# Two edits in a three-block model: modulation sums on VectorE alone, and relative biases written early from 128 partitions

## The chip, the cores and the metric

One core of one Trainium2 chip runs the whole program. The metric is the device time of one execution in microseconds, as the median of several runs. The engines that matter here are TensorE (PE, with its weight loads listed as PEld), VectorE (DVE), ScalarE (ACT), GpSimd (POOL) and the queues that issue transfers: SyncE (SP) for weights, and ACT's own queue for most other loads and stores.

## The reference, cut to what matters

A forward pass of three blocks over 256 tokens of width 1024. Two places of it bear on the change. The first block's attention adds to the scores of head h, query t and key s a bias that depends on the distance t - s alone, looked up in a table of 32 buckets by 8 heads. The third block is modulated by a vector `c` that doesn't depend on the tokens:

```
l_own = einsum('bhqd,bhkd->bhqk', qc, k_own) * scale + bias_h[:, t5_bucket(d_own)]   # block 1
logits = [where(d_own >= 0, l_own, NEG_INF)]
...
cond = silu(c)                                                                       # block 3, c: 1024
for layer in range(2):
    mod = cond @ ada_w[layer] + ada_b[layer]                                         # ada_w[layer]: 1024 x 6144
    shift1, scale1, gate1, shift2, scale2, gate2 = split(mod, 6)
    hn = rmsnorm(x, norm1_w[layer]) * (1 + scale1) + shift1
```

So the modulation is two products of a vector with a matrix of 1024 x 6144, 48 MB of weights in all. Its result is needed only in block 3, but it can be made at any time before.

## The kernel before, in words

Activations lie transposed, 128 features on the partitions, 256 tokens along the row. Nearly every weight matrix is loaded in chunks of 1 MB (128 x 2048 fp32, `wraw`, four buffers named raw, on SP's queue), and each half chunk is split by ACT into a rounded part `hi` (L316) and by DVE into the rest `lo` (L317), four buffers each. PE then does three matmuls of 256 columns for each product (L327 to L329), 48 a chunk. The program is written with a tile framework: each engine has one queue in order, and a scheduler fixes the order of each queue ahead of time. It goes by the order of the lines but may put an instruction ahead of earlier lines when, by its own reckoning, its inputs and its buffer are ready.

`mixers1` (L587) is the first half of block 1. It projects `va` in four chunks (L604 to L612), with the constants loaded at j = 2 (L609), normalises it (L613 to L630), projects `u` (L631 to L636), mixes positions in eight groups (L645 to L653), and then makes the biases (L656 to L668): one matmul picks for 8 heads, on 8 partitions, the 256 bias values by distance; DVE copies them into `bv`, whose tail holds -1e30; a DMA on ACT's queue writes that row of 383 values 128 times for each head into a scratch `relb` in memory; and a second DMA on the same queue reads `rel` (128 x 8 x 256) back with a step that shifts each partition's row by one, so that partition t sees the biases of query t. Then come four chunks each of q and k (L671 to L680), four of v (L681 to L686), and the attention, which first uses `rel` at L701. Large tiles of this stage share nine "wide" buffers of 8 KB per partition.

`peer` (L838) is the second half. Stage "route" selects experts (`chosen`, L859), writes the coefficients to the scratch `coef` and ends with `embed` (L907), which uses w_pp and w_pg. Stage "down" loops over 64 chunks of experts: `ex.down(j)` multiplies the hidden values `gel` with the coefficients (a `slab` is read from `coef` every four chunks, on ACT's queue), splits a chunk of peer_v and does 48 matmuls into four long sums; `ex.up(j + 18)`, as long as j < 46, does the same amount for a later chunk of peer_u; and `ada.step()` does one step of the modulation. Slabs and the accumulator `adaw` share four wide buffers.

`Modulation` (L1391): `start` (L1400) makes `cond` = silu(c) as 128 x 8 in a tile that is kept. There are 48 steps, one for each 1 MB of ada weights. A step loads 128 rows (inputs on the partitions) by 2048 outputs, and DVE adds weight times cond into `adaw` (L1413 for the first of eight, L1415 for the others). After eight steps the column sums are made by PE (`finish`, L1421): 16 matmuls with a block of 128 outputs of `adaw` as weights and a single column of ones, each in two passes of fp32, so 32 weight loads and 32 matmuls of one column (L1426). Six such finishes fill `mod`.

Of the kernel before, what the change touches and what calls it, by code (L numbers as in the profile page):

```python
# [12 lines left out]
F32 = mybir.dt.float32  # L13
# [3 lines left out]
AF = mybir.ActivationFunctionType  # L17
OP = mybir.AluOpType
# [5 lines left out]
D = 1024  # L24
KT = D // 128
NEG = -1e30
LOWEST = -3.0e38
WCH = 2048
# [18 lines left out]
class Pack:  # L47


    def __init__(self):  # L50
        self.parts, self.at, self.n = [], {}, 0
# [71 lines left out]
def tcol(v):  # L123

    return np.asarray(v).reshape(-1, 128).T
# [8 lines left out]
def prepare(**a):  # L134
    a = {k: np.asarray(v) for k, v in a.items()}
    d = {}
    vec = Pack()
    d["xT"] = lay(a["x"][0].T.reshape(D, T), T)[0]
    d["pT"] = lay(a["p"][0, 0].T.reshape(256, T), T)[0]
    w, b = a["w_in"][0], a["b_in"][0]  # L140
    for i, n in enumerate(("u", "va", "q", "k", "vb", "ga", "gb")):
        d["w_" + n] = lay(w[:, i * D:(i + 1) * D], 256)
        if n not in ("va", "vb"):
            vec.add("b_" + n, tcol(b[i * D:(i + 1) * D]))
    d["rows"] = np.stack([b[D:2 * D], b[4 * D:5 * D], a["gmlp_ln_g"][0], a["gmlp_ln_b"][0]])
    d["gm_ws"] = np.ascontiguousarray(a["gmlp_w_s"][0].transpose(2, 0, 1)).reshape(128, -1)
    d["gm_bs"] = a["gmlp_b_s"][0].reshape(1, -1)
    d["w_pa"] = lay(a["w_proj_a"][0], 256)
# [19 lines left out]
    w = a["nsa_w_in_2"][0]  # L168
    o = [0, 1024, 1280, 1536, 1792, 2048, 2304, 2560, 2608]
    q, kc, vc, ks, vs, kw, vw, g = (w[:, o[i]:o[i + 1]] for i in range(8))  # L170
# [13 lines left out]
    d["rows16"][0] = a["fox_b_f_2"][0]  # L184
    d["rows16"][1] = np.concatenate([a["m_i_bias_3"][0], a["m_f_bias_3"][0]])

    vec.add("c", tcol(a["c_3"][0]))
    for l in range(2):
        d[f"ada{l}"] = np.ascontiguousarray(a["ada_w_3"][l].reshape(KT, 128, 3, WCH).transpose(2, 0, 1, 3))
        vec.add(f"ada_b{l}", tcol(a["ada_b_3"][l]))  # L190
        vec.add(f"n1w{l}", tcol(a["norm1_w_3"][l]))
        vec.add(f"n2w{l}", tcol(a["norm2_w_3"][l]))
    vec.add("fnw", tcol(a["final_norm_w_3"]))
    w = a["m_w_in_3"][0]
# [22 lines left out]
class Core:  # L217
# [107 lines left out]
    def mm3(self, ps, w, x, start, stop, **k):  # L325
        mm = self.nc.tensor.matmul
        mm(ps, w[0], x[0], start=start, stop=False, **k)  # L327
        mm(ps, w[0], x[1], start=False, stop=False, **k)  # L328
        mm(ps, w[1], x[0], start=False, stop=stop, **k)  # L329
# [249 lines left out]
def block1(c, x, ada):  # L579
    with c.phase("mix1", 9):  # L580
        hs = mixers1(c, x)
    ada.start()
    with c.phase("peer", 0):
        return peer(c, x, hs, ada)


def mixers1(c, x):  # L587
    nc, d = c.nc, c.d
# [8 lines left out]
    def row(i, eng=nc.scalar):  # L597
        r = c.big([D], nm="row")
        src = d["rows"]
        eng.dma_start(r, bass.AP(tensor=src.tensor, offset=src.offset + i * D, ap=[[0, 128], [1, D]]))  # L600
        return r

    va = c.big([2, D], nm="va")
    for j in range(4):  # L604
        ps = c.tok_chunk(d["w_va"][j], xs, w=None if j else first)
# [4 lines left out]
        f = slice(j * 256, j * 256 + 256)  # L610
# [13 lines left out]
    nc.vector.tensor_scalar(sc[:, :, 3:4], sc[:, :, 3:4], -0.5, 1.5, op0=OP.mult, op1=OP.add)  # L624
    nc.vector.tensor_tensor(sc[:, :, 3:4], sc[:, :, 3:4], sc[:, :, 2:3], op=OP.mult)
    lg, lb = row(2), row(3)
    for i in range(2):
        nc.vector.tensor_scalar(va[:, i], va[:, i], st[:, i, 12:13], sc[:, i, 3:4], op0=OP.subtract, op1=OP.mult)
        nc.vector.tensor_tensor(va[:, i], va[:, i], lg, op=OP.mult)
        nc.vector.tensor_tensor(va[:, i], va[:, i], lb, op=OP.add)  # L630
    u = c.big([KT, T], nm="u")  # L631
    for j in range(4):
        ps = c.lin_chunk(d["w_u"][j], xs)
        for f in range(2):
            g = 2 * j + f
# [6 lines left out]
    src = d["gm_bs"]  # L642
    nc.scalar.dma_start(bs, bass.AP(tensor=src.tensor, offset=src.offset, ap=[[0, 128], [128, 8], [1, 128]]))
    a = (c.big([KT, T], F32R, nm="ahi"), c.big([KT, T], F32R, nm="alo"))
    for g in range(8):  # L645
        ps = c.ms_ps()[:, :256].rearrange("p (n t) -> p n t", n=2)
        for n in range(2):
            nc.tensor.matmul(ps[:, n], va[:, n, g * 128:g * 128 + 128], ws[:, g], start=True, stop=True)
        s = c.small([2, 128], tag="sg")
        nc.vector.tensor_tensor(s, ps, bs[:, g:g + 1, :].to_broadcast([128, 2, 128]), op=OP.add)  # L650
        s = s.rearrange("p n t -> p (n t)")
# [1 line left out]
        c.split(u[:, g], a[0][:, g], a[1][:, g])  # L653


    L = 383  # L656
    ps = c.ms_ps()
    nc.tensor.matmul(ps[:8, :256], c.V("rel_bias")[:32, :], c.C("onehot")[:32, :], start=True, stop=True)
    bv = c.small([384], tag="bv", bufs=1)
    nc.vector.memset(bv[:8, :], NEG)  # L660
    nc.vector.tensor_copy(bv[:8, :256], ps[:8, :256])
    scr = c.dr.tile([8, 128 * L], F32, name="relb")
    nc.scalar.dma_start(scr.rearrange("h (r l) -> h r l", l=L),
                        bv[:8, None, :L].to_broadcast([8, 128, L]))
    rel = c.big([8, 256], nm="rel")
    s = scr[:, :]
    nc.scalar.dma_start(rel, bass.AP(tensor=s.tensor, offset=s.offset + 127,
                                     ap=[[L - 1, 128], [128 * L, 8], [1, 256]]))  # L668


    q, k = c.big([KT, T], nm="q"), c.big([KT, T], nm="k")  # L671
    for j in range(4):
        ps = c.lin_chunk(d["w_q"][j], xs)
        for f in range(2):
            h = 2 * j + f
            nc.vector.tensor_scalar(q[:, h], ps[:, f], c.V("b_q")[:, h:h + 1], 128.0 ** -0.5, op0=OP.add, op1=OP.mult)
        ps = c.lin_chunk(d["w_k"][j], xs)
        for f in range(2):
            h = 2 * j + f
            nc.vector.tensor_scalar(k[:, h], ps[:, f], c.V("b_k")[:, h:h + 1], None, op0=OP.add)  # L680
    vb = c.big([2, D], nm="vb")  # L681
    bvb = row(1)
    for j in range(4):
        ps = c.tok_chunk(d["w_vb"][j], xs)
        f = slice(j * 256, j * 256 + 256)
        nc.vector.tensor_tensor(vb[:, :, f], ps, bvb[:, None, f].to_broadcast([128, 2, 256]), op=OP.add)  # L686
    o = (c.big([KT, T], F32R, nm="ohi"), c.big([KT, T], F32R, nm="olo"))
# [46 lines left out]
    for j in range(4):  # L734
        parts = []
        for gate, proj, src in (("ga", "pa", a), ("gb", "pb", o)):
            ps = c.lin_chunk(d["w_" + gate][j], xs)
            sg = c.small([2, 256], tag="sgm", bufs=3)
            for f in range(2):
                g = 2 * j + f  # L740
                nc.scalar.activation(sg[:, f], ps[:, f], AF.Sigmoid, bias=c.V("b_" + gate)[:, g:g + 1])
            ps = c.lin_chunk(d["w_" + proj][j], src)
# [5 lines left out]
    for j in range(5):  # L748
        if j < 4:
            ps = c.lin_chunk(d["w_o"][j], m, apart=j == 3)  # L750
# [87 lines left out]
def peer(c, h, hs, ada):  # L838

    scr = c.dr.tile([T // TB, 128, 128 * TB], F32, name="coef")  # L840
    ex = Experts(c, h, hs, scr)
    with c.phase("route", 2, ("r2", "gel")):
        chosen(c, h, hs, ex, scr)
    with c.phase("down", 4, ("r2", "gel")):
        for j in range(64):
            ex.down(j)
            if j + GELS < 64:
                ex.up(j + GELS)
            ada.step()
        mean = c.ms_ps()[:, :T]  # L850
        for b in range(4):
            w = h[:, 2 * b:2 * b + 2]
            c.nc.vector.tensor_tensor(w, w, ex.ys[b], op=OP.add)
            for f in range(2):
                c.rows_add(mean, w[:, f], b + f == 0, b + f == 4)
    return c.layer_norm(h, mean, c.V("ln2_g"), c.V("ln2_b"), c.V("ng00"))
# [534 lines left out]
class Modulation:  # L1391
# [1 line left out]


    def __init__(self, c, mod):
        self.c, self.mod = c, mod
        self.cond = c.keep.tile([128, KT], F32, name="cond")
        self.at, self.acc, self.late = 0, None, []

    def start(self):  # L1400
        self.c.nc.scalar.activation(self.cond, self.c.V("c"), AF.Silu)

    def step(self):
        c, nc = self.c, self.c.nc
        lg, k = divmod(self.at, KT)
        if lg < 6:
            self.at += 1
            l, g = divmod(lg, 3)
            w = c.wraw(c.d[f"ada{l}"][g, k])
            cond = self.cond[:, k:k + 1]  # L1410
            if k == 0:
                self.acc = c.big(nm="adaw")
                nc.vector.tensor_scalar(self.acc, w, cond, None, op0=OP.mult)  # L1413
            else:
                nc.vector.scalar_tensor_tensor(self.acc, w, cond, self.acc, op0=OP.mult, op1=OP.add)  # L1415
        while self.late:
            self.finish(*self.late.pop(0))
        if lg < 6 and k == KT - 1:
            self.late.append((l, g, self.acc))

    def finish(self, l, g, acc):  # L1421

        c, nc = self.c, self.c.nc
        cols = c.ms_ps()[:, :16]
        for i in range(16):
            nc.tensor.matmul(cols[:, i:i + 1], acc[:, i * 128:i * 128 + 128], c.C("one")[:, :1], start=True, stop=True)  # L1426
        o = 16 * g
        nc.vector.tensor_tensor(self.mod[:, l, o:o + 16], cols, c.V(f"ada_b{l}")[:, o:o + 16], op=OP.add)


def modulated(c, x, sums, w, scale, shift, out=None):
# [577 lines left out]
def build(nc, tc, dram, vec_at, out):  # L2009
    with ExitStack() as ctx:  # L2010
        c = Core(tc, ctx, dram, vec_at)
        x = c.keep.tile([128, KT, T], F32, name="x")
        mod = c.keep.tile([128, 2, 48], F32, name="mod")
        ada = Modulation(c, mod)
        sums, hs = block1(c, x, ada)
        sums = block2(c, x, sums, hs)
        block3(c, x, sums, mod, out)
# [22 lines left out]
```

## Time and profile before

| | us |
|---|---|
| median of 3 runs | 2997.18 (2993.87 to 3000.24) |
| the profiled execution, device time | 2989.64 |
| its span, first to last instruction | 2987.9 |
| PE busy in it | 2854.9 (96%) |
| DVE busy | 2060.0 (69%) |
| ACT busy | 1547.6 (52%) |

All stretches of time below are of the profiled execution. A busy share is an average over stages with different limits, so it is read stage by stage: the view by stretches gives each engine's busy time, the number of its instructions and the granted clock of TensorE in each stretch, and the views of waits and of time say which engine stood still and what ended it. A matmul's duration is longer than the distance to the next, since matmuls are pipelined; the count in a stretch gives the rate.

### The profile page before, as it was taken

To read this page: it belongs to the slowest core of one execution; us is meant where nothing else is said; L and a number is where in the kernel's file an instruction comes from. 1 tells how busy PE (TensorE), PEld (TensorE's weight loads), DVE (VectorE), ACT (ScalarE), POOL (GpSimd) and SP (SyncE) were. 2 spreads that over 40 slices of the span, in tenths; PEclk is the share of its full clock that TensorE was granted. 3 is DMA by queue.
4 is the path that set the end of the run, shared out by engine and by line. 5 is a ranking of instruction groups with operands and counts; after the bars stand their busy time and mean duration, and the time that the engine had idled before them with its cause. 6 is when DMAs were issued, how large, how long until landed. Compare 5 with 4: busy or idle time off the path is not lost. (4 is left out here: it accounts for less than half of the span.)

```text
span 2987.9 us, 51592 instructions
## 1 busy us (share of the span) xinstructions
PE 2854.9 (96%) x21106; PEld 2699.0 (90%) x21106; DVE 2060.0 (69%) x3625; ACT 1547.6 (52%) x2199; POOL 160.8 (5%) x136
## 2 busy tenths in 40 slices
PE   8799999899999999999999999989899999999998
PEld 8699988799999999987899989989899998788886
DVE  6365979776666676577555655555655696899997
ACT  5254417544444444437544464445544555777775
POOL 0000000000000000040000100000100071000000
PEclk9899999999999999999999999989999999999998
DMA  7544345677887796541354424534155432788885
GB/s 262 178 149 171 112 148 221 223 282 278 287 280 277 280 320 231 182 161 48 115 184 171 155 98 142 183 128 172 70 184 186 162 128 99 268 318 333 324 330 216
DMA packets 117709, 601.72 MB, mean 201 GB/s; under 512 B 9688, under 2 KB 45016, under 8 KB 48472
## 3 DMA queue, kind: packets, MB, share of 16 engines
q1 hardware_dynamic: 78480, 557.96, 52.1%
q10 hardware_dynamic: 38984, 40.39, 4.4%
q8 instruction: 167, 2.74, 0.4%
q14 instruction: 78, 0.64, 0.1%
HBM read 578.91 MB, written 19.39 MB: 200 GB/s over the span
## 5 line engine op out<-in xcount | busy, mean ns | idle before, releaser
L317 DVE TENSOR_TENSOR lo<-raw,hi 128x1024 fp32r<-128x1024 f32 x921 | 1130.8, 1243 | 639.0 <-ACT hi L316 635.4
L316 ACT ACTIVATE hi<-raw 128x1024 fp32r<-128x1024 f32 x921 | 966.9, 1057 | 1001.6 <-PE mm L328 519.5
L327 PE MATMUL mm<-nhi,hi 128*128 128x256 f32 x1312 | 379.5, 290 | 10.2 <-ACT nhi L491 6.8
L328 PE MATMUL mm<-nlo,hi 128*128 128x256 f32 x1312 | 379.6, 290 | 0.5 <-DVE nlo L492 0.5
L329 PE MATMUL mm<-nhi,lo 128*128 128x256 f32 x1312 | 377.3, 288 | 0.0
L329 PE MATMUL mm<-lhi,lo 128*128 128x256 f32 x1072 | 306.4, 286 | 8.3 <-DVE lo L317 8.3
L327 PE MATMUL mm<-lhi,hi 128*128 128x256 f32 x1072 | 305.9, 286 | 2.6 <-ACT lhi L454 2.3
L328 PE MATMUL mm<-llo,hi 128*128 128x256 f32 x1072 | 307.2, 287 | 0.0
L328 PE MATMUL ac<-r,hi 128*128 128x256 f32 x1024 | 294.0, 287 | 0.1
L327 PE MATMUL ac<-r,hi 128*128 128x256 f32 x1024 | 294.0, 288 | 0.0
L329 PE MATMUL ac<-r,lo 128*128 128x256 f32 x1024 | 293.3, 287 | 0.0
L327 PEld LDWEIGHTS mm<-nhi,hi 128*128 128x128 f32 x1312 | 258.5, 198 | 12.4 <-ACT nhi L491 7.6
L328 PEld LDWEIGHTS mm<-nlo,hi 128*128 128x128 f32 x1312 | 258.5, 197 | 2.4 <-DVE nlo L492 1.7
L329 PEld LDWEIGHTS mm<-nhi,lo 128*128 128x128 f32 x1312 | 258.3, 197 | 0.1
L329 PEld LDWEIGHTS mm<-lhi,lo 128*128 128x128 f32 x1072 | 207.6, 194 | 10.5 <-DVE lo L317 9.5
L327 PEld LDWEIGHTS mm<-lhi,hi 128*128 128x128 f32 x1072 | 207.7, 194 | 4.4 <-ACT lhi L454 2.9
L328 PEld LDWEIGHTS mm<-llo,hi 128*128 128x128 f32 x1072 | 207.5, 194 | 1.1 <-issue 0.7
L328 PEld LDWEIGHTS ac<-r,hi 128*128 128x128 f32 x1024 | 198.9, 194 | 0.3 <-DVE r L323 0.3
L329 PEld LDWEIGHTS ac<-r,lo 128*128 128x128 f32 x1024 | 198.7, 194 | 0.0
L327 PEld LDWEIGHTS ac<-r,hi 128*128 128x128 f32 x1024 | 198.7, 194 | 0.0
L328 PE MATMUL ac<-hlo,hi 128*128 128x256 f32 x688 | 193.0, 281 | 0.0
L327 PE MATMUL ac<-hhi,hi 128*128 128x256 f32 x688 | 192.8, 280 | 0.0
(592 smaller groups left out, 6285.3 us busy)
## 6 DMA issues: line engine op xcount, KB each, us to landing
raw<-in_moe_gu SPq DMA_DIRECT2D x88, 1024.0 KB, 6.1
raw<-in_peer_u SPq DMA_DIRECT2D x64, 1024.0 KB, 4.9
raw<-in_peer_v SPq DMA_DIRECT2D x64, 1024.0 KB, 5.1
raw<-in_ada SPq DMA_DIRECT2D x48, 1024.0 KB, 7.3
raw<-in_moe_d SPq DMA_DIRECT2D x40, 1024.0 KB, 6.2
raw<-in_up SPq DMA_DIRECT2D x32, 1024.0 KB, 4.9
raw<-in_down SPq DMA_DIRECT2D x32, 1024.0 KB, 4.9
raw<-in_ffn_gu SPq DMA_DIRECT2D x22, 1024.0 KB, 4.9
```

Source lines behind the costliest of these rows:

```text
L316: nc.scalar.activation(hi, raw[:, a:a + m], AF.Copy)
L317: nc.vector.tensor_tensor(lo, raw[:, a:a + m], hi, op=OP.subtract)
L327: mm(ps, w[0], x[0], start=start, stop=False, **k)
L328: mm(ps, w[0], x[1], start=False, stop=False, **k)
L329: mm(ps, w[1], x[0], start=False, stop=stop, **k)
```

## The change

The modulation's weights are laid out with outputs on the partitions: a load of 1 MB holds 2 x 128 outputs by 1024 inputs. `cond` becomes a row of 1024 values on every partition, read by a broadcast DMA on ACT's queue at the start of the down loop, followed by the silu. A step is two multiplications by that row, in place, each of which also sums along the row into one column of `mod`; ada_b is added once per layer. The column sums on PE, `adaw` and `finish` are gone. There are still 48 steps; they run at j = 2 to 49 instead of 0 to 47, and the stage has three wide buffers instead of four.

The biases are made right after the statistics of `va`, on 128 partitions: for each head a matmul whose weights are one column of the table repeated 128 times gives the 256 values on every partition, in four pairs; ACT copies each pair into `rows`. The values and a tile of -1e30 filled by POOL go to `relb`, now 128 x 8 x 383, in two DMAs on ACT's queue. The read of `rel` stands after the q and k chunks.

```diff
@@ prepare
-    d["rows"] = np.stack([b[D:2 * D], b[4 * D:5 * D], a["gmlp_ln_g"][0], a["gmlp_ln_b"][0]])
+    d["rows"] = np.stack([b[D:2 * D], b[4 * D:5 * D], a["gmlp_ln_g"][0], a["gmlp_ln_b"][0],
+                          np.asarray(a["c_3"][0]).reshape(-1)])
-    vec.add("c", tcol(a["c_3"][0]))
-        d[f"ada{l}"] = np.ascontiguousarray(a["ada_w_3"][l].reshape(KT, 128, 3, WCH).transpose(2, 0, 1, 3))
+        d[f"ada{l}"] = np.ascontiguousarray(a["ada_w_3"][l].reshape(D, 24, 2, 128).transpose(1, 3, 2, 0)).reshape(24, 128, WCH)
@@ block1
-    ada.start()
@@ mixers1, after the statistics of va
+    L = 383
+    rows, low = c.big([8, 256], nm="relw"), c.small([L - 256], tag="bv", bufs=1)
+    nc.gpsimd.memset(low, NEG)
+    for h in range(0, 8, 2):
+        ps = c.ms_ps().rearrange("p (h l) -> p h l", h=2)
+        for i in range(2):
+            nc.tensor.matmul(ps[:, i], c.V("rel_bias")[:32, h + i:h + i + 1].to_broadcast([32, 128]),
+                             c.C("onehot")[:32, :], start=True, stop=True)
+        nc.scalar.activation(rows[:, h:h + 2], ps, AF.Copy)
+    scr = c.dr.tile([128, 8, L], F32, name="relb")
+    nc.scalar.dma_start(scr[:, :, :256], rows)
+    nc.scalar.dma_start(scr[:, :, 256:], low[:, None, :].to_broadcast([128, 8, L - 256]))
@@ mixers1, after the mixing of positions
-    L = 383
-    ps = c.ms_ps()
-    nc.tensor.matmul(ps[:8, :256], c.V("rel_bias")[:32, :], c.C("onehot")[:32, :], start=True, stop=True)
-    bv = c.small([384], tag="bv", bufs=1)
-    nc.vector.memset(bv[:8, :], NEG)
-    nc.vector.tensor_copy(bv[:8, :256], ps[:8, :256])
-    scr = c.dr.tile([8, 128 * L], F32, name="relb")
-    nc.scalar.dma_start(scr.rearrange("h (r l) -> h r l", l=L),
-                        bv[:8, None, :L].to_broadcast([8, 128, L]))
-    rel = c.big([8, 256], nm="rel")
-    s = scr[:, :]
-    nc.scalar.dma_start(rel, bass.AP(tensor=s.tensor, offset=s.offset + 127,
-                                     ap=[[L - 1, 128], [128 * L, 8], [1, 256]]))
@@ mixers1, after the q and k chunks
+    rel = c.big([8, 256], nm="rel")
+    s = scr[:, :, :]
+    nc.scalar.dma_start(rel, bass.AP(tensor=s.tensor, offset=s.offset + 127, ap=[[8 * L - 1, 128], [L, 8], [1, 256]]))
@@ peer
-    with c.phase("down", 4, ("r2", "gel")):
+    with c.phase("down", 3, ("r2", "gel")):
+        ada.start()
...
-            ada.step()
+            if j > 1:
+                ada.step()
@@ Modulation.start
-        self.c.nc.scalar.activation(self.cond, self.c.V("c"), AF.Silu)
+        c, nc = self.c, self.c.nc
+        src = c.d["rows"]
+        self.cond = c.small([D], tag="cond", bufs=1)
+        nc.scalar.dma_start(self.cond, bass.AP(tensor=src.tensor, offset=src.offset + 4 * D, ap=[[0, 128], [1, D]]))
+        nc.scalar.activation(self.cond, self.cond, AF.Silu)
@@ Modulation.step (the old step and finish are gone)
+        if self.at == 48:
+            return
+        l, q = divmod(self.at, 24)
+        self.at += 1
+        w = c.wraw(c.d[f"ada{l}"][q]).rearrange("p (a k) -> p a k", a=2)
+        for i in range(2):
+            o = 2 * q + i
+            nc.vector.scalar_tensor_tensor(w[:, i], w[:, i], 1.0, self.cond, op0=OP.mult, op1=OP.mult,
+                                           accum_out=self.mod[:, l, o:o + 1])
+        if q == 23:
+            nc.vector.tensor_tensor(self.mod[:, l], self.mod[:, l], c.V(f"ada_b{l}"), op=OP.add)
```

## Rows read from the trace of the kernel before

Times are us from the span's start. A row of a stretch gives its bounds and length, then for PE, PEld, DVE, ACT and POOL the busy us and the number of instructions, then the granted clock as a share of full speed, the DMA share and GB/s. A row of waits says who waited for whom: us in total, times, longest. A row of time gives start, duration, engine, line, operation and count. A row of a group gives line, engine, operation, tiles and shapes, count, then busy us, mean ns of one, and idle us before it. A row of transfers gives count, KB each and us to landing.

**Rows 1.** The page's busy times.

```profile
PE 2854.9 (96%) x21106; PEld 2699.0 (90%) x21106; DVE 2060.0 (69%) x3625; ACT 1547.6 (52%) x2199; POOL 160.8 (5%) x136
```

**Rows 2.** Stretches of 20 us in mixers1.

```profile
40.00:60.00 20.00, 20.00 (x170) 19.96 (x168) 15.59 (x22) 12.28 (x19) 5.87 (x1) 1.00 0.65 246
...
80.00:100.00 20.00, 2.58 (x22) 2.38 (x20) 0.00 (x0) 0.00 (x0) 0.00 (x0) 0.62 0.46 98
100.00:120.00 20.00, 15.12 (x111) 14.83 (x112) 11.38 (x14) 8.13 (x8) 0.00 (x0) 0.79 0.74 253
120.00:140.00 20.00, 20.00 (x169) 20.00 (x168) 11.63 (x15) 7.41 (x7) 0.00 (x0) 1.00 0.56 201
```

**Rows 3.** Waits from 60 to 120 us.

```profile
ACT hi L316 <- DMA relb<-bv: 31.2, 1, 31.2
...
PE mm L327 <- ACT hi L316: 21.8, 1, 21.8
```

**Rows 4.** ACT in order of time, 66 to 106 us.

```profile
67.42 1.28 ACTq L663 DMA_DIRECT2D relb<-bv  x1
...
102.79 0.39 ACTq L667 DMA_DIRECT2D rel<-relb  x1
```

**Rows 5.** Stretches of the down loop, 40 us each, and 600 to 1130 as one.

```profile
620.00:660.00 40.00, 40.00 (x337) 40.00 (x336) 28.20 (x23) 18.39 (x21) 0.00 (x0) 1.00 0.75 272
680.00:720.00 40.00, 40.00 (x314) 40.00 (x313) 26.91 (x35) 14.76 (x18) 0.00 (x0) 0.91 0.81 281
...
880.00:920.00 40.00, 38.34 (x311) 38.13 (x310) 27.76 (x35) 15.52 (x18) 0.00 (x0) 0.96 0.74 262
...
1160.00:1200.00 40.00, 40.00 (x315) 40.00 (x314) 18.40 (x19) 15.01 (x18) 0.00 (x0) 0.91 0.44 155
600.00:1130.00 530.00, 528.34 (x4349) 528.13 (x4348) 367.65 (x376) 230.04 (x263) 0.00 (x0) 0.98 0.80 287
```

**Rows 6.** PE in order of time around one column sum.

```profile
696.06 4.12 PE L1426 MATMUL ms<-cst,adaw 128*128 128x1 f32 x32
...
700.40 0.41 PE L328 MATMUL ac<-r,hi 128*128 128x256 f32 x1
```

**Rows 7.** Waits from 584 to 1200 us.

```profile
DVE gel L978 <- DMA slab<-coef: 13.6, 6, 6.6
DVE adaw L1415 <- DMA raw<-in_ada: 12.2, 16, 2.1
...
PE mm L329 <- DVE lo L317: 2.1, 3, 1.7
```

**Rows 8.** A stretch of fp32 matmuls alone (L953), and ACT's copy of 128x512.

```profile
380.00:400.00 20.00, 20.00 (x94) 17.60 (x93) 1.00 0.42 144
...
L924 ACT ACTIVATE r<-mm 128x512 f32<-128x512 f32 x4 | 2.4, 598 | 2.5 <-PE mm L329 2.5
```

**Rows 9.** Transfers by line, us to landing last.

```profile
coef<-stg ACTq DMA_DIRECT2D x16, 1024.0 KB, 4.6
...
row<-in_rows ACTq DMA_DIRECT2D x3, 512.0 KB, 8.1
...
vecs<-in_vec SPq DMA_DIRECT2D x1, 496.0 KB, 13.0
```

**Rows 10.** Groups of DVE by line and shape.

```profile
L1415 DVE SCALAR_TENSOR_TENSOR adaw<-raw,cond,adaw 128x2048 f32<-128x2048 f32 x42 | 98.6, 2348 | 12.2 <-DMA raw<-in_ada 12.2
...
L1530 DVE SCALAR_TENSOR_TENSOR me<-ac,me 128x256 f32<-128x256 f32 x8 | 3.4, 424 | 2.8 <-ACT me L1524 2.7
L1678 DVE SCALAR_TENSOR_TENSOR lg<-hf,lg 128x1024 f32<-128x1024 f32 x2 | 2.4, 1220 | 1.1 <-ACT lg L1677 1.1
...
L1694 DVE TENSOR_TENSOR X<-bc,bk 128x512 f32<-128x512 f32 x1 | 2.1, 2069 | 0.0
L1530 DVE DVE_READ_ACCUMULATOR me<-ac,me 128x1 f32 x16 | 1.3, 83 | 0.0
```

**Rows 11.** Waits from 555 to 605 us.

```profile
DVE gel L978 <- DMA slab<-coef: 7.6, 2, 6.9
```

More of the change, by code (lines that the diff above doesn't have):

```diff
@@ L1395, in __init__ @@
     def __init__(self, c, mod):
-        self.c, self.mod = c, mod
-        self.cond = c.keep.tile([128, KT], F32, name="cond")
-        self.at, self.acc, self.late = 0, None, []
+        self.c, self.mod, self.at = c, mod, 0
     def start(self):
-        self.c.nc.scalar.activation(self.cond, self.c.V("c"), AF.Silu)
+        c, nc = self.c, self.c.nc
[3 more added lines that the diff above has]
+        nc.scalar.activation(self.cond, self.cond, AF.Silu)
     def step(self):
+        if self.at == 48:
+            return
         c, nc = self.c, self.c.nc
[L1405 to L1428, printed above, removed]
+        l, q = divmod(self.at, 24)
[7 more added lines that the diff above has]
+            nc.vector.tensor_tensor(self.mod[:, l], self.mod[:, l], c.V(f"ada_b{l}"), op=OP.add)
 def modulated(c, x, sums, w, scale, shift, out=None):
```

## The prediction

> **What bounds the kernel now.** The first view is the page's table of busy times [rows 1]. TensorE (PE) is busy for 96% of the span, so the question is where its missing time and its slow clock lie, and whether the change touches those places. It touches two stretches: the first 160 us (mixers1) and 560 to 1200 us (the loop over 64 expert chunks, "down").
>
> Mixers1: the view by stretches of 20 us [rows 2]. At full rate PE does 169 matmuls in 20 us, 0.118 us each. Between 80 and 120 us it does 22 + 111 = 133 where 338 would fit: 205 are missing, 205 x 0.118 = 24.3 us. Granted clock 0.62 and 0.79 there means that part of the stretch ran at the lower of its two levels (1.2 instead of 2.4 GHz), after PE had stood still; the count of missing matmuls holds that loss too. The waits of 60 to 120 us [rows 3] say who held it: PE waited 21.8 us for ACT's casts of weights, and ACT 31.2 us for the transfer `relb<-bv`. The timeline of ACT [rows 4] gives the order: the write of `relb` is issued at 67.4 us, two casts follow, and then the read `rel<-relb`, next on the same queue, is issued at 102.8 us only. The write took some 35 us for 1.5 MB, from 8 partitions. A table that is used only after the q, k and v projections holds up all casts behind it.
>
> The down loop: the view by stretches of 40 us [rows 5]. The undisturbed one (620 to 660) holds 337 matmuls, 0.119 us each. Six others hold one column sum of the modulation each (L1426, 32 weight loads and matmuls of one column, [rows 6]); the first and the last stand in the group. Take 32 off the count of each, and 282, 295, 279, 282, 295 and 283 are left: 55, 42, 58, 55, 42 and 54 short, together 306, or 36.3 us. In the third PE was also idle for 1.7 us, so 34.6 us belong to the column sums: six times some 4 us are their own time, the rest is clock. Behind the 32 matmuls of one column those of 256 columns stand 0.21 us apart instead of 0.12, from 700.4 us [rows 6] for 26 matmuls, and the granted clock of the stretch is 0.91 [rows 5]. PE's own waits in the whole loop are 2.1 us [rows 7]: it is the bound there; VectorE (DVE), busy 367.7 of 530 us [rows 5], is not.
>
> **The change, part by part.** (a) *Early biases.* Gone: one matmul in two passes, a small copy, the write from 8 partitions, and with it the stall of 24.3 us. New on PE: 8 matmuls of fp32, two passes of 256 columns each. An fp32 pass of 256 columns takes 0.213 us (94 in 20 us, [rows 8]): 16 x 0.213 = 3.4 us, less 0.4 for the two removed passes: 3.0 us, on PE's path, since PE has no gap from 40 to 60 us [rows 2]. New on ACT: 4 copies of 128x512 at 0.60 us [rows 8], 2.4 us, and two DMA issues. ACT is busy 12.3 us of 20 there [rows 2], and its casts have buffers ahead, so their own time costs nothing; without that cover it would be those 2.4 us. But two PSUM buffers serve the four pairs, so PE can wait for a copy that sits behind a cast: 0 to 2.4 us, taken as 2. If the scheduler puts the matmuls ahead of the landing of the vectors (13.0 us after their issue, [rows 9]), PE stands for them: 0 to 13 us; taken as 0, since three chunks of va come first in the program. The fill of `low` goes to POOL, busy 5.9 of 20 us there: nothing.
>
> The write is of the same 1.5 MB, now from 128 partitions in rows of 1 KB and 508 B. The nearest row is `coef<-stg`, 1 MB from 128 partitions, 4.6 us to landing [rows 9]; the far end is the 35 us of before. It lies beside the loads of weights (DMA share 0.65, [rows 2]); up to four buffers ahead cover these. The read now stands behind the last k chunk in the program, on ACT's queue, with the casts behind it if the write were still under way: even at the far end a write issued at 45 us is done by 80, before the q and k chunks are. The four vb chunks (48 matmuls, 5.7 us each) lie between the read and the first use of `rel`. So the stall goes, and nothing is late next: the casts behind it are paced by PE as at 120 to 140 us. Sum of (a): 24.3 - 3.0 - 2 = 19.3 us gained.
>
> (b) *Modulation on DVE alone.* Gone from PE: the 34.6 us worked out above. Gone from DVE: 42 x 2.348 us (L1415) and six plain products, put at L1678's 1.22: 105.9 us [rows 10]. New on DVE: 96 multiply-and-sum over 128x1024. A scalar_tensor_tensor over 128x1024 takes 1.220 us (L1678); one with a sum over its row takes the time of its elements (L1530, 424 ns for 256), plus 83 ns to read the sum out [rows 10]: 96 x 1.303 = 125.1 us, 19.2 more than before (the two additions of ada_b are below 1 us). Over the 530 us of [rows 5] DVE goes from 69% to 73%; the cover is DVE's own idle time. No row shows such a sum with both sources in SBUF (L1530 reads one from PSUM), so its price is bounded: below by 1.22, above by the slowest line with two sources, L1694, 2.07 us for 512 elements, or 4.14 for 1024. I take 1.30, by the nearer form; L1694 reads a repeated operand in short pieces.
>
> A rule of the Trainium skill speaks against that value: the page "Vector Engine (DVE) Microarchitecture Reference", section 7 "Points that are easy to get wrong", says that a scalar_tensor_tensor with two SBUF sources that aren't bf16 runs at half throughput, as both read ports are taken and none is left for the accumulator. Without a sum the rows contradict half rate (L1678: two sources in SBUF, 1.220 us for 1024 elements); with a sum no row here decides, so it is a rival below.
>
> (c) *The start of the loop.* The silu over 128x8, done early beside other work, becomes a broadcast DMA of 512 KB on ACT's queue and a silu over 128x1024 at the head of the loop. The stretch is a weak one already: DVE stood 6.9 us there for the first slab, and PE behind DVE [rows 11]. ACT now waits for the broadcast (8.1 us to landing for the same shape, `row<-in_rows`, [rows 9]), then for one or two table loads and some 1 us of work; behind it in ACT's queue stand the issues of slabs and the casts for w_pg and the first experts, and behind those DVE and PE. Much of this lies in the 6.9 us in which DVE stands anyway. Bounds: nothing, and 8.1 + 4 = 12 us; I take 4, a third, because two waits of the same length overlap. The two steps moved from j = 0, 1 to j = 48, 49 take along, on SP's queue, two loads of 1 MB with their buffers and, on DVE, 2 x 2.6 us; at j = 48 a chunk has only 48 matmuls (5.7 us) and one load of its own, and DVE's work per chunk is about half of the 5.7 us that it has before (below), so 2.9 + 2.6 = 5.5 us still fit: 0; without that fit 2 x 2.6. Three wide buffers instead of four serve slabs alone, since adaw had held one: 0.
>
> Sum: 19.3 + 34.6 - 4 = 49.9 us. The profiled execution took 2989.6 us (span 2987.9); the median of the runs is 2997.2, their spread 6.4. 2989.6 - 49.9 = 2939.7 for an execution like the profiled one; for the median, which I predict, 2997.2 - 49.9 = 2947.
>
> **The rivals.** *Half-rate sums.* 530 us are 46.5 chunks of 96 x 0.119 = 11.4 us; DVE's 367.7 us less 46.5 x 2.21 for the modulation leave 5.7 us of other work a chunk. If a sum costs the 2.35 us of 2048 elements today, a pair costs 4.87, together 10.6 of 11.4 us: DVE at 93%, and the 12.2 + 13.6 us for which it waits for transfers in the loop [rows 7] find little slack. Taking half of these 26: 2947 + 13 = 2960. The skill's rule gives the same price. Against it: L1415 and L1678 have full rate.
>
> *The stall moves.* ACT again stands in its queue, for `relb` (if the scheduler issues the read right behind a write that still takes 35 us) or for the broadcast at 560 us with all that is behind it. Price: most of (a)'s 24 us, 2971. For it: loads stand where the scheduler puts them, and ACT's queue waits in order [rows 4]. Against it: 16 times the partitions, and the rows of `coef`.
>
> *Loads become the bound, and PE's saved time turns into waits.* 287 GB/s in the loop [rows 5]; for 6% less time 305. Against it: the waits for loads [rows 7] are DVE's, not of casts for u and v. Half of (b) lost: 2964.
>
> *Slower than before: DVE becomes the bound.* Place: the 48 steps of the loop. With x us a sum, a chunk costs DVE 5.7 + 2(x + 0.083); it exceeds PE's 11.4 from x = 2.8, and from x = 3.0 the excess, 48 x 0.5 us, and the 26 us of transfers eat the whole 50. At L1694's rate, x = 4.14: 48 x 2.7 + 26 = 156, 2997 - 50 + 156 = 3103. Against it: every other row.
>
> *It doesn't do what it says* for the clock: if the level falls for another reason, some 34.6 - 24 = 11 us of (b) stay away: 2958.
>
> **How the numbers follow.** Forecast 0.69, clock unchanged 0.05, half-rate sums 0.09, stall moved 0.08, loads 0.05, slower 0.04. The range takes in the bounds of (a) and (c), the half-rate and the clock case: upward 8 for the broadcast, some 6 for the vectors, 13 for half rate and 6 for the spread of the runs, not all at once: 2968. Downward, (c) at nothing, the copies at nothing and some of the dip at 560 us gone, with the spread: 2934. 0.2% (6 us) is about what a measurement of this kernel can tell from no change. All cases but the last are faster, some of their tails not by 6 us: 0.93 faster, 0.03 same, 0.04 slower.
>
> **What would show it.** (a): no wait of ACT for `relb`, 169 matmuls per 20 us from 80 to 120 us at clock 1.00. (b): sums near 1.22 + 0.08 us, no granted clock below 0.98 in stretches of 40 us from 620 to 1200, 337 matmuls in each. (c): one wait of ACT for cond near 560 us, under 9 us. It would be wrong if PE waited for lo in the loop for more than 10 us, if ACT stood for `relb` or cond for over 10, or if PE stood near 20 us for the constants.

## The result, and the profile after

The changed kernel takes 2943.1 us (median of 4 runs, 2939.3 to 2946.6), the kernel before 2995.5 us beside it: a ratio of 0.9825, 95% interval 0.9804 to 0.9847, or 52 us less. The forecast was 2947, the range 2934 to 2968.

The profiled execution of the changed kernel has a span of 2942.3 us, 45.6 less than that of before. Three marks in both traces say where the 45.6 went: the first softmax operation that uses `rel`, the first addition behind the down loop (L853 before, L855 after), and the end.

| us | before | after | difference |
|---|---|---|---|
| start to first use of `rel` | 156.6 | 137.5 | -19.1 |
| from there to the end of the down loop | 1101.0 | 1068.9 | -32.1 |
| from there to the end (code unchanged) | 1730.3 | 1735.9 | +5.6 |

The busy times, as in [rows 1]: PE has 28 us less, DVE 9.6 us more.

```profile
PE 2826.9 (96%) x20928; PEld 2671.7 (91%) x20928; DVE 2069.6 (70%) x3763; ACT 1551.0 (53%) x2203; POOL 157.1 (5%) x137
```

Mixers1, the same view as [rows 2] (columns: stretch, length, then busy us and instructions of PE, PEld, DVE, ACT, POOL, granted clock, DMA share, GB/s):

```profile
20.00:40.00 20.00, 20.00 (x146) 19.15 (x146) 13.32 (x15) 9.40 (x12) 0.00 (x0) 0.94 0.90 356
40.00:60.00 20.00, 20.00 (x163) 19.54 (x162) 14.28 (x21) 12.39 (x17) 1.10 (x1) 1.00 0.76 260
...
80.00:100.00 20.00, 20.00 (x169) 20.00 (x168) 11.35 (x14) 7.30 (x8) 0.00 (x0) 1.00 0.77 272
100.00:120.00 20.00, 20.00 (x169) 20.00 (x169) 11.62 (x14) 7.13 (x8) 0.00 (x0) 1.00 0.57 204
```

The stretch from 80 to 120 us, which held 133 matmuls, now holds 338 at full clock. The price is paid earlier: from 20 to 60 us there are 309 matmuls, 339 before. ACT in order of time (start, duration, engine, line, operation) shows the queue that stood before [rows 4]:

```profile
1.04 0.62 ACTq L638 DMA_DIRECT2D relb<-bv  x1
...
43.10 0.52 ACTq L637 DMA_DIRECT2D relb<-relw  x1
...
79.22 0.39 ACTq L680 DMA_DIRECT2D rel<-relb  x1
82.08 1.06 ACT L316 ACTIVATE hi<-raw 128x1024 fp32r<-128x1024 f32 x1 [1.82 <-PE mm L328]
```

The values are written at 43.1 us (6.3 us to landing), the fill of -1e30 (the tile bv) was even put first of all, and the cast behind the read of `rel` waits for PE and not for a transfer.

The down loop behind its start, one stretch, to be set beside the last of [rows 5]:

```profile
580.00:1120.00 540.00, 540.00 (x4529) 540.00 (x4528) 402.27 (x534) 250.48 (x288) 0.00 (x0) 1.00 0.83 297
```

4529 matmuls in 540 us, 0.119 us each, without a dip of the clock: before, the same view had 4349 in 530 us at 0.98, some 160 of them of one column. DVE's sums (line, operation, shapes, count, then busy us, mean ns, idle before), to be set beside [rows 10], and the waits from 560 to 1160 us beside [rows 7]:

```profile
L1416 DVE SCALAR_TENSOR_TENSOR raw<-raw,cond 128x1024 f32<-128x1024 f32 x96 | 113.9, 1221 | 13.0 <-DMA raw<-in_ada 12.6 <-DVE lo L317 0.2
L1416 DVE DVE_READ_ACCUMULATOR raw<-raw,cond 128x1 f32 x96 | 8.0, 83 | 0.0
```

```profile
DVE raw L1416 <- DMA raw<-in_ada: 12.6, 17, 2.8
...
PE mm L329 <- DVE lo L317: 3.3, 1, 3.3
```

A sum over 1024 elements with both sources in SBUF takes 1.221 us and 83 ns to read out, as forecast. DVE still waits 12.6 us for ada loads; from 580 us on PE notices none of it. The 3.3 us of PE lie ahead of that, at 571 us, and come up again under E7.

### The profile page after: what moved, and what is told of

The parts are those of the page before. It is cut to its first block, busy times and chain, and to the rows that moved or that the text cites. A ratio compares the mean times of both kernels' runs of the same rounds, so it can differ in the third digit from the quotient of the medians.

```text
span 2942.3 us, 51410 instructions
## 1 busy us (share of the span) xinstructions
PE 2826.9 (96%) x20928; PEld 2671.7 (91%) x20928; DVE 2069.6 (70%) x3763; ACT 1551.0 (53%) x2203; POOL 157.1 (5%) x137
## 5 line engine op out<-in xcount | busy, mean ns | idle before, releaser
L328 PE MATMUL ac<-r,hi 128*128 128x256 f32 x1024 | 288.2, 282 | 0.0
L327 PE MATMUL ac<-r,hi 128*128 128x256 f32 x1024 | 287.7, 281 | 0.0
L328 PEld LDWEIGHTS ac<-r,hi 128*128 128x128 f32 x1024 | 192.9, 188 | 0.0
L329 PEld LDWEIGHTS ac<-r,lo 128*128 128x128 f32 x1024 | 192.7, 188 | 0.0
L327 PEld LDWEIGHTS ac<-r,hi 128*128 128x128 f32 x1024 | 192.7, 188 | 0.0
```

## The experiments

All are timed against the kernel before on the same chip; each ratio has its 95% interval. The first use of `rel` is what the expectations call "first soft". "Loop" is the time from it to the end of the down loop in the profiled execution, "rest" the time from there to the end.

| kernel | first use of `rel` | loop | rest | median, before beside it | ratio |
|---|---|---|---|---|---|
| before | 156.6 | 1101.0 | 1730.3 | | |
| changed | 137.5 | 1068.9 | 1735.9 | 2943.1, 2995.5 | 0.9825 (0.9804 to 0.9847) |
| E1 biases only | 138.2 | 1100.7 | 1737.7 | 2977.8, 2992.3 | 0.9954 (0.9940 to 0.9967) |
| E2 modulation only | 156.5 | 1070.4 | 1736.3 | 2966.8, 2992.3 | 0.9919 (0.9903 to 0.9936) |
| E3 one column, loose | 137.3 | 1094.3 | 1730.1 | 2971.6, 2992.3 | 0.9938 (0.9920 to 0.9956) |
| E4 wide, loose | 139.0 | 1078.3 | 1736.5 | 2954.2, 2992.3 | 0.9873 (0.9854 to 0.9891) |
| E5 early, 8 partitions | 153.4 | 1071.8 | 1730.2 | 2956.8, 2995.8 | 0.9875 (0.9852 to 0.9897) |
| E6 late, 128 partitions | 139.7 | 1070.6 | 1735.7 | 2942.5, 2995.8 | 0.9821 (0.9801 to 0.9842) |
| E7 cond behind slabs | 137.9 | 1070.1 | 1730.8 | 2942.5, 2995.8 | 0.9825 (0.9805 to 0.9846) |
| E8 sums twice | 138.0 | 1073.6 | 1735.7 | 2951.5, 2995.8 | 0.9861 (0.9837 to 0.9886) |
| E9 one column, tied | 137.6 | 1109.1 | 1734.6 | 2978.8, 2993.0 | 0.9943 (0.9927 to 0.9960) |
| E10 wide, tied | 138.2 | 1091.6 | 1733.5 | 2964.2, 2993.0 | 0.9904 (0.9887 to 0.9920) |
| E11 two slab buffers | 138.1 | 1071.2 | 1737.5 | 2945.5, 2993.0 | 0.9835 (0.9819 to 0.9852) |
| E12 steps from 0 | 138.8 | 1069.0 | 1734.5 | 2947.6, 2993.0 | 0.9854 (0.9836 to 0.9873) |

### E1 and E2: each part alone

E1 is the kernel before with the part of the diff in mixers1; E2 is the changed kernel with that part undone:

```diff
 E1: before, and
+    rows, low = c.big([8, 256], nm="relw"), ...          # after the statistics of va
-    ps = c.ms_ps(); matmul 8 rows; bv; scr; rel           # after the mixing of positions
+    rel = ...; nc.scalar.dma_start(rel, ...)              # after the q and k chunks
 E2: changed, and the same three in reverse
```

> The kernel before with the early biases alone; the modulation is as before. Theory (two separate gains: 19 us in mixers1, 33 us in the down loop): first soft at 137 to 139 us instead of 156.6, last sum of the down loop (1257.6 before) at 1238 to 1240, time 2995 - 19 = 2976. Rival (the stall in mixers1 only filled the buffers that the later stage then used, so its removal is given back): first soft at 138, but the end of the down loop at 1248 or later, time 2986 or more.

> The changed kernel with the biases as before (one matmul, 8 partitions, late): the modulation alone. Theory: first soft at 156 to 157 us, the stall of 31 us of ACT for relb back, the end of the down loop at 1257.6 - 33 = 1225, time 2962. Rival (the two parts need each other): time more than 6 us off 2962.

In the stages each part gives its own share and nothing is given back up to the end of the loop: E1 18.4 us before the first use of `rel` and 0.3 in the loop, E2 0.1 and 30.6. Together 49.4 of the 51.2 us of the changed kernel. The times say less: 14.5 and 25.5 us add up to 40, not 52. In the profiled executions, where the gap is 9.6 us, most of it lies behind the loop, where the code of all kernels is the same; the section on the prediction comes back to it.

### E3 and E4: column sums put back, first try

```diff
+        if self.at % 8 == 0:          # after every eighth step
+            cols = c.ms_ps()[:, :16]
+            for i in range(16):
+                nc.tensor.matmul(cols[:, i:i + 1], c.C("ident"), c.C("one")[:, :1], start=True, stop=True)
             ... (a copy of cols into a scrap tile)
 E4 instead: 9 times nc.tensor.matmul(ps[:, :256], c.C("ident"), c.cst[:, :256], start=True, stop=True)
```

> The changed kernel, with 16 matmuls of one column (32 passes, weights: a constant) after every eighth step of the modulation, their result unused. Theory (the column sums themselves cost 36 us, 24 by their own time and 12 by the clock): the end of the down loop 36 us later than in the changed kernel (1206 + 36 = 1242), granted clock 0.91 to 0.96 in six stretches of 40 us, time 2943 + 36 = 2979. Rival (the old finishes cost because TensorE waited for the accumulator or DVE's order was disturbed): own time only, 24 us or less, 2967, clock 1.00.

> The changed kernel, with 9 fp32 matmuls of 256 columns (18 passes of 0.213 us, 3.8 us) at the same six places, result unused: the own time of the column sums without their single columns. Theory (the level of the clock falls because single columns leave the engine's array nearly unused): 6 x 3.8 = 23 us later than the changed kernel, 2966, clock 1.00 in the loop. Rival (any break in the stream of split matmuls lets the level fall): 35 us later, 2978, clock below 0.97 in six stretches.

Neither tells the theories apart. These matmuls read only constants, so the scheduler put nearly all of them far ahead: in E3 all 192 run from 495 to 575 us, in E4 they lie between 497 and 1139, most of them ahead of 580. E9 and E10 are the same with weights that depend on the step.

### E9 and E10: the same, tied to the step

```diff
+            t = c.small([128], tag="extra")
+            nc.vector.tensor_copy(t, w[:, 1, :128])       # the step's own product
+            ... nc.tensor.matmul(cols[:, i:i + 1], t, c.C("one")[:, :1], ...)   # E9, 16 times
+            ... nc.tensor.matmul(ps, t, c.cst[:, :256], ...)                    # E10, 9 times
```

> As the first try with 16 matmuls of one column after every eighth step, but their weights are now a copy (128x128) of the step's own product, so that they can't run before the step: one at about every 91 us of the loop. Theory (the column sums cost TensorE 36 us: 24 by their own time, 12 by the clock): first soft to the end of the loop 1069 + 30 to 36 us = 1099 to 1105 instead of 1068.9, granted clock 0.83 to 0.96 in the stretches of 20 us behind them, time 2943 + 33 = 2976. Rival (only their own time): 24 us or less, 1093, clock 1.00, 2967.

> The same six places and the same copy, but 9 fp32 matmuls of 256 columns (18 passes of 0.21 us, 3.8 us each place). Theory (single columns leave the array nearly unused and the clock falls for that): own time alone, 6 x 3.8 = 23 us: first soft to the end of the loop 1092, clock 1.00 from 600 to 1150, time 2943 + 23 = 2966. Rival (any stretch of other work between the split matmuls lets the level fall): 1102 or more, clock below 0.97 behind the six places.

One of the six places in each kernel, the stretch and the one behind it, first E9, then E10:

```profile
980.00:1000.00 20.00, 20.00 (x146) 20.00 (x145) 11.09 (x17) 6.31 (x7) 0.00 (x0) 0.83 0.79 299
1000.00:1020.00 20.00, 20.00 (x170) 20.00 (x169) 15.19 (x20) 9.43 (x11) 0.00 (x0) 1.00 0.84 287
```

```profile
980.00:1000.00 20.00, 20.00 (x155) 19.53 (x155) 11.14 (x15) 7.74 (x9) 0.00 (x0) 1.00 0.86 303
1000.00:1020.00 20.00, 20.00 (x170) 20.00 (x169) 15.67 (x22) 9.40 (x11) 0.00 (x0) 1.00 0.78 284
```

E10 makes the loop 1091.6 - 1068.9 = 22.7 us longer, which is 6 x 3.8: own time and nothing else, clock 1.00. E9 makes it 40.2 us longer, more than the 30 to 36 expected, and the clock is 0.83 in the stretch shown, 0.83 to 0.93 at all six places: 17.5 us more than E10, in time 2978.8 against 2964.2. E9's six blocks take 3.7 to 4.9 us each by the trace, 26.2 together, which leaves some 14 us for the clock behind them. So not every break in the stream of split matmuls was followed by a fall of the clock: behind 32 weight loads with one column each it fell, behind 18 passes of 256 columns it stayed at 1.00. Whether the number of weight loads or the single column makes the difference is not told apart by these runs.

### E5 and E6: place or partitions

E5 keeps the early place and goes back to 8 partitions; E6 keeps the 128 partitions and goes back to the late place:

```diff
 E5: after the statistics of va
-    rows, low, 8 matmuls, 4 copies, two DMAs from 128 partitions
+    one matmul (8 x 256), bv on 8 partitions, scr [8, 128 * 383], one DMA
 E6: rows, low, 8 matmuls, 4 copies, both DMAs and the read of rel
-    after the statistics of va / after the q and k chunks
+    after the mixing of positions, ahead of the q and k chunks
```

> The changed kernel, with the biases made early but by the old means: one matmul, one write of 1.5 MB from 8 partitions, the read after the q and k chunks. Theory (the place of the write is what matters, since 35 us fit between 43 us and the read at 79): no wait of ACT for relb above 3 us; TensorE saves 14 passes of 0.21 us, ACT four copies, and the start its DMA of the fill: first soft at 132 to 136 instead of 137.5, time 2943 - 4 = 2939. Rival (the 128 partitions are what matters): ACT stands for relb for 15 us or more, first soft at 145 or later, time 2950 or more.

> The changed kernel, with the eight matmuls, the copies, the write from 128 partitions and the read at the place of before, behind the mixing of positions. Theory: the write lands in 6 to 10 us, ACT stands for it 3 to 7 us, the buffers of casts cover most of that: first soft at 137 to 142 instead of 156.6 before and 137.5 in the changed kernel, time 2943 to 2948. Rival (only the place matters, a write of 1.5 MB in short rows is slow): ACT stands 15 us or more, first soft at 150 or later, time 2955.

E6 came out as expected, but for the 3 to 7 us for which ACT was to stand: the write of the values (L666) lands in 7.9 us, the read is issued (L670) right behind that, the cast after it waits for PE and not for the write, and the time is that of the changed kernel.

```profile
72.53 0.54 ACTq L666 DMA_DIRECT2D relb<-relw  x1
75.54 1.06 ACT L316 ACTIVATE hi<-raw 128x1024 fp32r<-128x1024 f32 x1 [3.04 <-PE mm L328]
78.42 1.06 ACT L316 ACTIVATE hi<-raw 128x1024 fp32r<-128x1024 f32 x1 [1.82 <-PE mm L328]
80.48 0.40 ACTq L670 DMA_DIRECT2D rel<-relb  x1
81.30 1.06 ACT L316 ACTIVATE hi<-raw 128x1024 fp32r<-128x1024 f32 x1 [1.82 <-PE mm L328]
```

E5 went against its theory, and not quite by its rival either: ACT never stood for `relb`, yet the first use of `rel` came at 153.4 us. Its DMA issues (count, KB, us to landing) and waits up to 160 us:

```profile
ws<-in_gm_ws ACTq DMA_DIRECT2D x1, 512.0 KB, 27.8
```

```profile
POOL ws L650 <- DMA ws<-in_gm_ws: 75.5, 1, 75.5
...
PE ms L659 <- POOL ws L650: 12.5, 1, 12.5
```

The write from 8 partitions, issued at 36.7 us, is followed on the same queue by the load of `ws`, which POOL masks for the mixing of positions. That load, 3.5 us to landing in the kernel before, took 27.8, its issue alone 4.6 us, and PE waited 12.5 us for it. Moved early, the slow write found another victim. The transfers on SP's queue beside it were slow as well: weight loads of 1 MB took 9.5 to 19.1 us to landing in E5 and 19.2 to 19.6 in the kernel before, against 5.0 to 6.5 in the changed kernel from 50 to 62 us.

What removes the stall is the write from 128 partitions: E6 has 16.9 of the 19.1 us. The early place adds at most the other 2.2, little more than the 1.7 us by which this mark differs among the ten kernels with the new biases at the new place (137.3 to 139.0), and nothing in the time (0.9825 and 0.9821). One thing goes along with the partitions: the fill leaves by itself at the start, so the late write of E6 has 1.0 MB instead of 1.5. By bytes alone 35 us would become some 23, an estimate; it took 7.9.

### E8: DVE's slack

```diff
+            scrap = c.small([1], tag="scrap")
+            nc.vector.scalar_tensor_tensor(w[:, i], w[:, i], 1.0, self.cond, op0=OP.mult, op1=OP.mult,
+                                           accum_out=scrap)         # a second time
```

> The changed kernel, with each multiply-and-sum done a second time into a scrap: 96 more of 1.30 us, 125 us more on DVE, which is the price that half-rate sums would have had. Theory (DVE has 5.7 + 5.2 = 10.9 us of work a chunk against TensorE's 11.4, TensorE stays the bound): the end of the loop 0 to 15 us later than 1206.4, time 2943 to 2958, DVE busy 0.95 in the loop. Rival (DVE is already the bound in places, since it waits for loads): 30 us or more later.

```profile
580.00:1120.00 540.00, 539.55 (x4511) 539.15 (x4511) 491.81 (x708) 247.90 (x286) 0.00 (x0) 1.00 0.82 294
```

DVE is busy 491.8 us of 540, 91%, and the loop is 4.7 us longer than in the changed kernel, 1.8 longer than in E5, whose loop is the changed kernel's; the median is 9 more than those of E6 and E7 beside it. So the half-rate sums of the rival, with about as much DVE time, can be put at 2 to 9 us (an estimate from this run), not 13: DVE's waits for loads hide behind PE for the most part.

### E7, E11 and E12: the start of the loop

```diff
 E7: ada.start() in the loop, at j == 1, instead of ahead of it
 E11: with c.phase("down", 2, ...) instead of 3
 E12: ada.step() at every j again, instead of from j = 2
```

> The changed kernel, with the load of cond and its silu placed in the loop behind the first chunk (j = 1) instead of ahead of it. Theory (at the start of the loop the load of cond goes ahead of the first slab, DVE waits for the slab 8.5 us instead of 6.9, and TensorE waits for DVE): the slab's wait back at 7 us, the end of the loop 2 to 4 us earlier (1203 instead of 1206.4), time 2940. Rival (the dip at the start is the slab's own, as in the kernel before): the end of the loop within 1 us of 1206.4.

> The changed kernel with two wide buffers in the down loop instead of three. What it tells apart: why 540 to 580 us lost 13 us of TensorE where the kernel before lost 9. Theory (with adaw gone, slabs have three buffers to themselves, eight slabs of 1 MB are read in the first 60 us, and DVE does their products ahead of the casts that TensorE waits for): fewer slabs in that stretch, first soft to the end of the loop 3 to 5 us shorter than 1068.9. Rival (the two steps moved out of the start let DVE run ahead, whatever the buffers): no more than 1 us shorter, or longer.

> The changed kernel with the steps of the modulation at j = 0 to 47 as before. Theory of the buffers: the start of the loop no better, 1069 to 1072 from first soft to the end of the loop. Rival (the moved steps let DVE run ahead with products of slabs): the start as before, 3 to 5 us shorter, 1064 to 1066, fewer than five slabs read before 600 us.

None of the three shortens the loop: 1070.1, 1071.2 and 1069.0 us against 1068.9. The theories of E7 and E11, which expected 2 to 5 us, missed; in E12 the theory that expected no gain held, and the moved steps are out as a cause. The first 40 us of the loop hold 224 matmuls in the changed kernel and 261 in E1, whose modulation is the old one (stretch, length, busy us and instructions as above; first the changed kernel, then E1):

```profile
540.00:580.00 40.00, 29.89 (x224) 29.49 (x224) 24.75 (x46) 18.80 (x25) 0.00 (x0) 0.87 0.92 292
```

```profile
540.20:580.20 40.00, 33.99 (x261) 32.98 (x261) 24.61 (x37) 18.75 (x26) 0.00 (x0) 0.91 0.78 263
```

That is 37 matmuls, 4.4 us, lost at the start of the loop in the changed kernel. E2, with the old biases, has it too (220), so it comes with the modulation. But it isn't the load of cond: in E7, which puts the slab first and whose DVE waits 6.9 us for it as before, the count is 223. It isn't the number of buffers (E11, 212) nor the moved steps (E12, 217).

What the trace of the changed kernel shows there, ACT and then DVE in order of time:

```profile
541.77 0.34 ACTq L1404 DMA_DIRECT2D cond<-in_rows  x1
542.13 0.46 ACTq L973 DMA_DIRECT2D slab<-coef  x1
...
548.31 0.38 ACTq L973 DMA_DIRECT2D slab<-coef  x1
548.50 1.06 ACT L1405 ACTIVATE cond<-cond 128x1024 f32<-128x1024 f32 x1
```

```profile
552.00 0.76 DVE L980 TENSOR_TENSOR gel<-gel,slab 128x256 f32<-128x256 f32 x2 [8.46 <-DMA slab<-coef]
...
555.35 1.76 DVE L980 TENSOR_TENSOR gel<-gel,slab 128x256 f32<-128x256 f32 x5
557.03 1.22 DVE L317 TENSOR_TENSOR lo<-raw,hi 128x1024 fp32r<-128x1024 f32 x1
558.16 1.09 DVE L980 TENSOR_TENSOR gel<-gel,slab 128x256 f32<-128x256 f32 x3
```

The second slab is read at 548 us, 6 us behind the first; in the kernel before it came 21 us behind it. DVE does products of later chunks ahead of casts that PE waits for (6.8 us the longest wait, 5.2 before).

Most of the loss comes later than that. Up to 568 us the changed kernel has 166 matmuls and E1 171; from 568 to 580 us it has 60 and E1 92. There PE stands a second time, 3.3 us, for casts that DVE does only behind a product that waited for the fourth slab:

```profile
573.12 0.42 DVE L980 TENSOR_TENSOR gel<-gel,slab 128x256 f32<-128x256 f32 x1 [1.98 <-DMA slab<-coef]
573.46 4.62 DVE L317 TENSOR_TENSOR lo<-raw,hi 128x1024 fp32r<-128x1024 f32 x4
```

E2, E7, E11 and E12 have this second stand too (3.5, 4.3, 3.2 and 4.2 us; in E12 DVE waits there for an ada load), the kernel before and E1 have 0.3 us in its place. E7 does bring its first stand back to 5.2 us and has 173 matmuls up to 568 us, but loses at the second what it gained (52 matmuls there). All kernels with the new modulation but E3, whose start is full of the added matmuls, have the second slab 6 to 10 us behind the first; E11, meant to hold it back, didn't (548.6 us). Whether the early slabs are the cause was not tested by an otherwise undisturbed kernel that has the new modulation and a late second slab, and stays open.

## Why the prediction was right

*The bound and the two stalls.* Right. The wait of ACT for `relb` is gone and 80 to 120 us hold 338 matmuls, as many as the sum assumed.

*(a), 19.3 us: measured 19.1* in the changed kernel, 18.4 in E1. The 5 us of costs were right in sum, with other parts than given, and that is luck. The 16 fp32 passes run from 36.7 to 41 us, 3.4 us as reckoned. The 2 us for PE waiting on copies did not occur; ACT waited for PE. Instead the start is late, which the prediction had not seen: the scheduler put the fill of `relb` (508 KB in rows of 508 B) as the first DMA of all, at 1.04 us, among the first weight loads. It took 15.4 us to land, and PE's first matmul comes at 8.2 us instead of 6.5. The eleven kernels with this fill do 49 to 63 matmuls in the first 20 us; the three without it (before, E2, E5) do 69. The clock is 0.64 from 18 to 22 us, behind a wait of PE of 1.5 us for a `lo`, where the kernel before, with a wait of 1.8 us at the same place, had 1.00; but that fall doesn't go with the fill, since E1 has the fill without the fall and E5 the fall without the fill. The mechanism behind the gain was told too broadly: the text gave the stall to the 8 partitions and to the place, and let both count. E5 and E6 show that the write from 128 partitions does it, at the old place too, and that the early place alone gains 3.2 us (153.4 instead of 156.6).

*(b), 34.6 us.* The loop runs at 0.119 us a matmul with clock 1.00 throughout. The loop's 32.1 us, plus the 4.4 us lost at its start, are 36.5: the 36.3 of all six column sums, 34.6 without the idle 1.7 us. E9 gives it from the other side: putting single-column sums back costs 40.2 us, some 26 of own time and 14 of clock, where the text had 24 and 11.

*The price of a sum, 1.30 us.* Measured 1.221 + 0.083. The rule of the Trainium skill that was weighed against it ("Vector Engine (DVE) Microarchitecture Reference", section 7, half throughput for two SBUF sources that aren't bf16) isn't borne out here as the prediction read it: 1024 fp32 elements from two SBUF sources, with a sum, take the time that they take without one [rows 10]. The prediction went too far, though, where it said that the rows contradict half rate even without a sum. That hangs on what full rate is: the kernel before multiplies a tile by one value per partition, and that took about as long for twice the elements.

```profile
L1413 DVE TENSOR_SCALAR adaw<-raw,cond 128x2048 f32<-128x2048 f32 x6 | 7.7, 1282 | 0.2 <-DMA raw<-in_ada 0.2
```

*(c), 4 us: right in size, wrong in mechanism, so the size is luck.* The start of the loop did lose 4.4 us. But ACT did not stand for the broadcast: it landed 6.5 us after its issue at 541.8, ACT had casts and a table load to do meanwhile, and the silu followed at 548.5. What the load did was to hold up the first slab: DVE waited 8.5 us for it instead of 6.9 and PE 6.8 instead of 5.2. E7 undoes that and gains nothing in the end. Most of the loss, 32 of 37 matmuls, is the second stand at 571 us, behind DVE's products of slabs, which the prediction had at nothing.

*What the sum left out.* The rest of the kernel, whose code is unchanged, took 1730.3 us in the profiled execution of before and 1735.9 in that of the changed kernel; over all fourteen profiles it lies between 1730.1 and 1737.7, in no order that follows the edits. The rows below show one place, 1.2 of the 5.6 us: the same stage transition in the kernel before and in the changed kernel.

```profile
1640.00:1660.00 20.00, 16.28 (x105) 15.54 (x104) 12.67 (x28) 9.64 (x21) 5.15 (x5) 0.74 0.30 106
1660.00:1680.00 20.00, 20.00 (x167) 18.80 (x166) 14.04 (x24) 12.07 (x20) 4.74 (x5) 1.00 0.48 160
```

```profile
1589.00:1609.00 20.00, 16.28 (x115) 15.64 (x114) 12.04 (x28) 10.06 (x20) 1.93 (x2) 0.85 0.46 159
1609.00:1629.00 20.00, 19.43 (x147) 18.37 (x147) 13.06 (x22) 11.12 (x19) 9.03 (x7) 0.90 0.32 104
```

PE stands there in both; the clock returns after it at another point, and 272 matmuls become 262 in 40 us. The stretch behind the loop is also where E1 and E2 mostly fail to add up in their profiled executions: their spans are 11.3 and 24.7 us shorter than that of before, 36.0 together, where the changed kernel has 45.6. Of the 9.6 us between, 1.8 lie up to the end of the loop and 7.8 behind it (1737.7 and 1736.3 us there). That the gap of the medians has the same place is likely but not shown, since there is one profile of each kernel.

The stages themselves gained 51.2 us against 49.9 in the sum. That the median came within 4 us of the forecast is partly luck: the same 51.2 us became 45.6 in the profiled execution and 52 in the medians.

## What to carry to other kernels

A store or load that nobody needs soon can hold up others, whether that is an instruction behind one that waits for it (`relb`) or another transfer (`ws` in E5): make it short, here by spreading it over 128 partitions, before looking for a better place. Work on TensorE in single columns cost twice here, by its time and by the clock of the matmuls behind it; a sum that VectorE has room for was better made there. And when single stages are compared by marks in the trace, effects of some 3 us can be told that the total doesn't show: the two marks moved by 1.7 us (first use of `rel`) and 2.9 us (the loop) among kernels with the same code there, the stretch behind them by 7.6.

## What the runs showed of the hardware that was not expected

A write of 1.5 MB from 8 partitions, some 35 us long, went with slow transfers on both queues: on its own 27.8 us to landing for 512 KB that took 3.5 us otherwise, and 4.6 us for the issue instruction instead of 0.33 (E5); on SP's 19.2 to 19.6 us for weight loads of 1 MB (the kernel before) that took 5.0 to 6.5 in the changed kernel. A transfer of 508 KB in rows of 508 B took 15.4 us beside the first weight loads. And behind 16 fp32 matmul passes with weights on 32 partitions only, 0.21 us each, the clock stayed at 1.00, while behind 32 passes of a single column on 128 partitions it was 0.83 to 0.93 (E9, stretches of 20 us).
